# Sums for the modulation vectors on DVE: an order edge on every sum, and a wider spacing

## The chip, the core and the metric

The kernel runs on one NeuronCore of a Trainium2 chip. Time is device time in microseconds of one execution. The engines are named as in the profile: PE (TensorE, matmuls), PEld (its weight loads), DVE (VectorE), ACT (ScalarE), POOL (GpSimd), SP (SyncE, which here only issues DMAs). Each engine works through its own queue in the order in which the program was built, and waits for semaphores where an operand comes from another engine.

## What is computed

Two transformer blocks of two layers each, on 512 tokens of width 1024, in float32. What matters here is the feed-forward sublayer of the first block and the modulation vectors of the second:

```
def _swiglu(h, w_in, w_out):                       # first block, layers 0 and 1
    gu = h @ w_in
    return (jax.nn.silu(gu[..., :FFN_HIDDEN]) * gu[..., FFN_HIDDEN:]) @ w_out

# second block, for its layers l = 0, 1:
sc, sc_ctx = jax.nn.silu(c), jax.nn.silu(c_ctx)
mod   = split_cols((sc @ w_mod[l] + b_mod[l])[:, None, :], (D_MODEL,) * N_MOD)
mod_x = split_cols(sc_ctx @ w_mod[l] + b_mod[l], (D_MODEL,) * N_MOD)
```

FFN_HIDDEN is 2816, N_MOD is 6. The modulation of the second block depends on `c` and `c_ctx` alone, not on the tokens, so it may be computed at any earlier time. `w_mod[l]` is 1024 x 6144.

## The kernel before, in words

**The feed-forward sublayer** (`ffn_core`). The 2816 hidden columns are 22 tiles of 128, in three groups of 8, 8 and 6. For a tile `j`, PE multiplies two slabs of weights (gate and up, each split into a high and a low part, `whia`/`wloa` or `whib`/`wlob`) with the activations `xh`, `xl`: 48 matmuls into one PSUM buffer `b` of 128 x 1024. There are two such buffers. `post` then makes the hidden values: ACT takes a tanh of the gate half into `th`, DVE makes `(th + 1) * gate` (`scalar_tensor_tensor`) and `th * up` (`tensor_mul`), and after the second the PSUM buffer is free (`psB.rel`). So PE can start tile `j + 2` only when both DVE operations of tile `j` are done. ACT and POOL then split `th` into `hh` and `hl`. Behind the tiles of a group comes the product with the output weights, in two halves `h` of 512 columns, four token blocks each, in the same PSUM buffers; DVE adds the results to `x` (`evac`, seen as `x<-b,x`), and PE's second half needs the buffers of the first.

**The modulation** (`modulation`). Layer `l` of it runs as a stream of its own beside the feed-forward sublayer of layer `l` of the first block. It does not use PE for its large product: for each of six vectors `j`, and each of eight slabs of 128 rows of `w_mod` (512 KB each, loaded by ACT's DMA queue into one of three buffers `mw`), DVE multiplies the slab with one value of `c` per partition and adds it to the accumulator `macc` (128 x 1024). The first slab of a vector is a `tensor_scalar`, the other seven are a `scalar_tensor_tensor`; here they are called sums, all of them. For layer 0 both `c` and `c_ctx` are wanted for all vectors (96 sums), for layer 1 both for the first two and one for the rest (64 sums). Then the accumulator is reduced: a blockwise transpose (`mtr`), a reduction (`mpart`), a small matmul on PE (`s<-mpart,quart`), and an addition into `modc` or `mcol`. The load of slab `i` can only be issued when the sums on slab `i - 3` have released their buffer, and it is issued by ACT, whose queue also holds the casts of the feed-forward weights and the tanh.

**What sets the order.** The program is recorded by a small planner (`Weave`). Each stream is a generator; it is stepped when its planned time `ready` lies behind PE's planned time. An engine operation in a stream adds its estimated cost to `ready`, and the code may add to it by hand: behind each sum stands `w.cur.ready += 1800` (ns), which spreads the sums. After recording, a scheduler places the instructions of every engine in a final order; there, instructions of other streams may move past each other if nothing ties them. `with self.tc.issue_after(ins)` adds such a tie: what is recorded in the block stands behind `ins` in its engine's queue, without a semaphore. Before the change this tie is on the first slab of a vector alone (`k == 0`), and the instruction is the one that `self.normed` held when the stream began: the last subtraction of the normalisation that fills `xh` and `xl` (`split_T`, `self.normed = nc.vector.tensor_sub(...)`). All engine operations go through one helper, so the profile gives the line of that helper, L138, for all of them; operations are told apart by the names of their tiles.

Of the kernel before, what the change touches and what calls it, by code (L numbers as in the profile page):

```python
# [13 lines left out]
ALU = mybir.AluOpType  # L14
# [368 lines left out]
class Build:  # L383
# [765 lines left out]
    def ffn_core(self, wi, wo, segs, pre, setup, evac, nxt, grid=None):  # L1149
# [3 lines left out]
        nc, w, v = self.nc, self.w, self.nc.vector  # L1153
# [13 lines left out]
        def post(j, kk, pb, px, hs):  # L1167
            rth = mem["th"]
            th = yield from rth.take()
            ps = [(pb[:, :512], pb[:, 512:], slice(0, 512))]  # L1170
            if px is not None:
                ps.append((px[:, :256], px[:, 256:], slice(512, 768)))
            for pg, _, t in ps:
                nc.scalar.activation(th[:, t], pg, AF.Tanh, scale=0.5)
            yield
            for pg, _, t in ps:
                v.scalar_tensor_tensor(th[:, t], th[:, t], 1.0, pg, ALU.add, ALU.mult)
            for _, pu, t in ps:
                v.tensor_mul(th[:, t], th[:, t], pu)
            self.psB.rel()  # L1180
            if px is not None:
                self.psM.rel()
            yield
            for (hh, hl), (_, _, t) in zip(hs, ps):
                oh, ol, s = hh[:, kk], hl[:, kk], th[:, t]
                if grid is not None:
                    g = "p (c s n) -> p n s c", "p (n s c) -> p n s c"
                    g = g if grid == "to" else g[::-1]
                    oh, ol = (x.rearrange(g[0], s=2, n=4) for x in (oh, ol))
                    s = s.rearrange(g[1], s=2, n=4)  # L1190
                nc.scalar.copy(oh, s)
                self.sub(ol, s, oh.bitcast(F32), "pool")
            rth.rel()
# [14 lines left out]
        def units(js, gi, k0, cuts):  # L1208
            pbs = [(self.psB.get(), self.psM.get() if len(segs) > 1 else None) for _ in js]
            sl = {}  # L1210
            end = cuts[-1][1]
            for c0, c1, need in cuts:
                w.join(*need)
                for j, (pb, px) in zip(js, pbs):
                    for half, m in enumerate("gu"):
                        if (m, j) not in sl:
                            sl[m, j] = self.slabs.get(wi, (m, j))
                        self.mm_a(sl[m, j], outs(half, pb, px, c0, c1))
                        if c1 == end:
                            self.slabs.done(sl[m, j])  # L1220
                    if c1 == end:
                        posts[j] = w.spawn(post(j, j - k0, pb, px, hidden(gi)), 0)
# [4 lines left out]
        for gi, (k0, n) in enumerate(FFN_GROUPS):  # L1227
# [13 lines left out]
            for h in range(1 if last else 2):  # L1241
                acc = self.accs(nb)
# [92 lines left out]
    def modulation(self, l, pool, after):  # L1335

        nc, A, v, w = self.nc, self.A, self.nc.vector, self.w
        for s in after:
            yield s
        normed = self.normed  # L1340
        bm = pool.tile([128, 6, 8], F32, name="bm", tag="bm", bufs=1)
        nc.scalar.dma_start(bm, A["bmod_col"][l])
        wm = {}

        def load(i):
            if i < 48:
                j, k = divmod(i, 8)
                wm[i] = pool.tile([128, 1024], F32, name="mw", tag="mw", bufs=3)
                t = w.cur.ready
                nc.scalar.dma_start(wm[i], A["w_mod"][l, k * 128:k * 128 + 128,  # L1350
                                                      j * 1024:j * 1024 + 1024])
                w.cur.ready = t

        load(0)
        load(1)
        w.cur.ready += 5000
        for j in range(6):
            n_v = 2 if l == 0 or j < 2 else 1
            acc = pool.tile([128, 2, 1024], F32, name="macc", tag="macc", bufs=1)
            for k in range(8):  # L1360
                load(8 * j + k + 2)
                wt = wm.pop(8 * j + k)
                for s in range(n_v):
                    cs = self.cv[:, s, k:k + 1]
                    if k == 0:
                        with self.tc.issue_after(normed.ins):
                            v.tensor_scalar(acc[:, s], wt, cs, None, ALU.mult)
                    else:
                        v.scalar_tensor_tensor(acc[:, s], wt, cs, acc[:, s], ALU.mult, ALU.add)
                    w.cur.ready += 1800  # L1370
                    yield
            w.cur.ready += 5000
            yield

            part = pool.tile([128, 2, 32], F32, name="mpart", tag="mpart", bufs=1)
            for s in range(n_v):
                tr = pool.tile([128, 1024], F32, name="mtr", tag="mtr", bufs=1)
                v.transpose(tr, acc[:, s])
                yield
                v.tensor_reduce(part[:, s], tr.rearrange("p (i q) -> p i q", q=32), AX.X, ALU.add)  # L1380
                yield
            n = 8 * n_v
            pt = yield from self.psS.take()
            ps = pt[:, :n].rearrange("p (s k) -> p s k", s=n_v)
            for q in range(4):
                nc.tensor.matmul(ps[32 * q:32 * q + 32], self.quart,
                                 part[:, :n_v].rearrange("p s (k q) -> p q s k", q=4)[:, q],
                                 start=True, stop=True)
            yield
            if j in (2, 5):  # L1390
                col = pool.tile([128, 2, 8], F32, name="mcol", tag="mcol", bufs=1)
                v.tensor_add(col[:, :n_v], ps, bm[:, j].unsqueeze(1).to_broadcast([128, n_v, 8]))
                yield
                nc.tensor.transpose(pt[:n, 128:256], col[:, :n_v].rearrange("p s k -> p (s k)"), self.ident)
                yield
                gr = pool.tile([16, 128], F32, name="gr", tag="gr", bufs=1)
                nc.scalar.copy(gr[:n], pt[:n, 128:256])
                self.psS.rel()
                yield
                nc.scalar.dma_start(self.grow[l, j // 3, :n_v].rearrange("s (k c) -> (s k) c", k=8), gr[:n])  # L1400
                yield
            else:
                jj = {0: 0, 1: 1, 3: 2, 4: 3}[j]
                for s in range(n_v):
                    v.scalar_tensor_tensor(self.modc[:, l, jj, s], ps[:, s], 1.0 if jj % 2 else 0.0,
                                           bm[:, j], ALU.add, ALU.add)
                self.psS.rel()
                yield
# [1167 lines left out]
```

## Time and profile before

| | |
|---|---|
| median of 3 runs | 3430.48 us (3426.53 to 3433.2) |
| profiled execution | 3435.41 us, its span 3433.6 us |
| PE busy | 3123.7 us, 91% of the span |
| DVE busy | 1735.3 us, 51% |
| ACT, POOL busy | 1257.0 us (37%), 1440.1 us (42%) |
| mean granted clock of TensorE | 0.947 |
| chain of waits | PE 67%, DVE 23%; `macc` alone 5% |
| all sums with their opening products | 270.5 us of DVE: 140 of 1812 ns, 20 of 1166 ns |

The span runs from the first to the last instruction. The feed-forward sublayer of layer 0 begins at about 440 us of it, that of layer 1 at about 1210 us. DVE is busy for half of the span on average, but in 440 to 640 us for 179.0 of 200 us. A busy share of PE counts matmuls whose ends are modelled; a wait is read from the idle time in front of an instruction, and what ended it.

### The profile page before, as it was taken

What the parts mean: (1) busy time and instruction counts of PE and PEld (TensorE: products, weight loads), DVE (VectorE), ACT (ScalarE), POOL (GpSimd) and SP (SyncE); (2) the same over time, 40 slices, a digit from 0 to 9 for tenths busy, and PEclk for the clock granted to TensorE, in tenths of its full rate; (3) what the DMA queues carried; (4) which work ended last, traced back from release to release, by engine and by line L of the source; (5) the groups of instructions that cost most, each with busy time, mean ns of one, the idle gap of its engine ahead of it and who ended that gap; (6) DMA issues with size and microseconds to landing.
All of it is one profiled execution on the core that took longest, in us unless ns stands there. A gap on an engine that the chain in (4) does not pass through costs nothing.

```text
span 3433.6 us, 44377 instructions
## 1 busy us (share of the span) xinstructions
PE 3123.7 (91%) x16596; PEld 2696.9 (79%) x16596; DVE 1735.3 (51%) x4221; ACT 1257.0 (37%) x2542; POOL 1440.1 (42%) x987
## 2 busy tenths in 40 slices
PE   7889888999999979999899897999998799869998
PEld 5678767777998767788788777888886789758886
DVE  6975598543464697213644755121015855751113
ACT  4443322222454422333455635212122555543322
POOL 2313344554323245555523325434445534355555
PEclk9989989999999989999999899999999899889999
DMA  3111255432222267323101212111111111242221
GB/s 106 63 33 62 87 178 172 158 122 95 68 63 68 74 210 244 124 94 118 51 24 44 74 41 80 62 65 65 62 67 53 52 39 54 66 122 94 98 98 68
DMA packets 99449, 301.82 MB, mean 88 GB/s; under 512 B 18673, under 2 KB 26017, under 8 KB 99233
## 3 DMA queue, kind: packets, MB, share of 16 engines
q1 hardware_dynamic: 74000, 236.36, 20.3%
q10 hardware_dynamic: 25232, 62.62, 5.7%
q8 instruction: 131, 2.15, 0.3%
q14 instruction: 86, 0.70, 0.1%
HBM read 290.98 MB, written 7.95 MB: 87 GB/s over the span
## 4 chain that ended last, share of the span: by engine, by line
PE 67%; DVE 23%; issue 4%; ACT 3%; DMA 2%; POOL 1%; ACTq 0%; SPq 0%; DVEq 0%; POOLq 0%
PE b L138 37%; PE m L138 24%; PE s L138 6%; DVE macc L138 5%; DVE rs_t L138 4%; DVE x L138 2%; DVE four L138 1%; ACT xn L138 1%; DMA mw<-w_mod 1%; DVE w2k L138 1%; DVE qrs L138 1%; DVE cx L138 1%; DVE tmp L138 1%; DVE T L138 1%; DVE th L138 1%
## 5 line engine op out<-in xcount | busy, mean ns | idle before, releaser
L138 POOL TENSOR_TENSOR wloa<-wrawa,whia 128x1024 fp32r<-128x1024 f32 (+2 forms) x164 | 391.9, 2391 | 617.8 <-ACT whia L138 375.3
L138 DVE SCALAR_TENSOR_TENSOR th<-th,b 128x512 f32<-128x512 f32 x88 | 60.3, 685 | 720.3 <-ACT th L138 720.3
L138 POOL TENSOR_TENSOR wlob<-wrawa,whib 128x1024 fp32r<-128x1024 f32 (+1 forms) x123 | 297.7, 2423 | 301.2 <-ACT whib L138 191.2
L138 ACT CAST whia<-wrawa 128x1024 fp32r<-128x1024 f32 (+2 forms) x164 | 168.3, 1027 | 401.8 <-PE b L138 162.0
L138 PE MATMUL b<-xh,whib 128*128 128x512 f32 (+1 forms) x768 | 288.6, 381 | 24.2 <-DVE th L138 16.8
L138 PE MATMUL b<-xh,whia 128*128 128x512 f32 (+1 forms) x768 | 286.7, 379 | 14.1 <-DVE th L138 12.1
L138 PE MATMUL b<-xl,whia 128*128 128x512 f32 (+1 forms) x768 | 285.2, 377 | 2.0 <-POOL xl L138 2.0
L138 PE MATMUL b<-xl,whib 128*128 128x512 f32 (+1 forms) x768 | 286.7, 379 | 0.0
L138 DVE SCALAR_TENSOR_TENSOR macc<-mw,cv,macc 128x1024 f32<-128x1024 f32 x140 | 247.9, 1812 | 16.1 <-DMA mw<-w_mod 15.6
L138 ACT CAST whib<-wrawa 128x1024 fp32r<-128x1024 f32 (+1 forms) x123 | 125.7, 1022 | 327.8 <-PE b L138 164.5
L138 POOL TENSOR_TENSOR wloa<-wrawb,whia 128x1024 fp32r<-128x1024 f32 (+2 forms) x61 | 141.6, 2321 | 189.5 <-ACT whia L138 120.2
L138 PE MATMUL m<-xh,whia 128*128 128x512 f32 (+2 forms) x520 | 188.3, 367 | 23.6 <-DVE T L138 10.1
L138 POOL TENSOR_TENSOR wlob<-wrawb,whib 128x1024 fp32r<-128x1024 f32 (+1 forms) x61 | 149.8, 2456 | 131.3 <-ACT whib L138 85.4
L138 POOL TENSOR_TENSOR hl<-th,hh 128x512 fp32r<-128x512 f32 (+1 forms) x110 | 151.8, 1389 | 101.4 <-ACT hh L138 97.0
L138 PE MATMUL b<-xh,wlob 128*128 128x512 f32 (+1 forms) x768 | 194.0, 373 | 0.0
L138 PE MATMUL b<-xh,wloa 128*128 128x512 f32 (+1 forms) x768 | 192.2, 372 | 0.0
L138 PE MATMUL m<-xl,whia 128*128 128x512 f32 (+2 forms) x520 | 184.9, 360 | 3.0 <-POOL xl L138 2.9
L138 PEld LDWEIGHTS b<-xh,whib 128*128 128x128 f32 x768 | 148.0, 193 | 47.3 <-issue 11.9
L138 PEld LDWEIGHTS b<-xh,whia 128*128 128x128 f32 x768 | 147.1, 191 | 36.4 <-issue 13.6
L138 PE MATMUL m<-whib,xh 128*128 128x512 f32 (+3 forms) x432 | 162.6, 379 | 13.8 <-ACT xh L138 12.8
L138 PE MATMUL m<-whia,xh 128*128 128x512 f32 (+3 forms) x440 | 170.8, 392 | 4.6 <-ACT xh L138 2.8
L138 PE MATMUL m<-whia,xl 128*128 128x512 f32 (+3 forms) x440 | 167.3, 383 | 0.4 <-DVE xl L138 0.3
(459 smaller groups left out, 8025.7 us busy)
## 6 DMA issues: line engine op xcount, KB each, us to landing
mw<-w_mod ACTq DMA_DIRECT2D x96, 512.0 KB, 4.3
wrawa<-ffn_w_in SPq DMA_DIRECT2D x60, 512.0 KB, 3.3
wrawa<-w_ffn_in SPq DMA_DIRECT2D x56, 512.0 KB, 3.3
wrawa<-gdn_w_in SPq DMA_DIRECT2D x32, 512.0 KB, 3.3
wrawb<-w_ffn_in SPq DMA_DIRECT2D x32, 512.0 KB, 3.3
wrawa<-w_ffn_out SPq DMA_DIRECT2D x32, 512.0 KB, 3.3
wrawb<-ffn_w_in SPq DMA_DIRECT2D x28, 512.0 KB, 3.3
wrawa<-ffn_w_out SPq DMA_DIRECT2D x28, 512.0 KB, 3.3
```

Of the source, the lines that this page charges most:

```text
L138: r = f(*a, **k)
```

## The change

It does two things, both in `modulation`, with one line in `ffn_core` for it. `self.normed` is now also set by the `tensor_mul` on `th` in `post`, so it always names the newest such product (or the normalisation's subtraction, before the first); and every sum, not only the first of a vector, is recorded behind what `self.normed` holds at that moment. And the time that the planner adds behind each sum is 2300 ns in place of 1800.

```
             for _, pu, t in ps:
-                v.tensor_mul(th[:, t], th[:, t], pu)
+                self.normed = v.tensor_mul(th[:, t], th[:, t], pu)
...
-        normed = self.normed
...
                     cs = self.cv[:, s, k:k + 1]
-                    if k == 0:
-                        with self.tc.issue_after(normed.ins):
+                    with self.tc.issue_after(self.normed.ins):
+                        if k == 0:
                             v.tensor_scalar(acc[:, s], wt, cs, None, ALU.mult)
-                    else:
-                        v.scalar_tensor_tensor(acc[:, s], wt, cs, acc[:, s], ALU.mult, ALU.add)
-                    w.cur.ready += 1800
+                        else:
+                            v.scalar_tensor_tensor(acc[:, s], wt, cs, acc[:, s], ALU.mult, ALU.add)
+                    w.cur.ready += 2300
```

DVE at the first tiles of the feed-forward sublayer of layer 0, before (`macc<-mw,cv` is the opening product of a vector, `macc<-mw,cv,macc` a sum; the two operations on `th<-th,b` are those of `post`):

```order
L138 TENSOR_SCALAR macc<-mw,cv 128x1024 x2
L138 SCALAR_TENSOR_TENSOR macc<-mw,cv,macc 128x1024 x9
L138 SCALAR_TENSOR_TENSOR th<-th,b 128x512
L138 SCALAR_TENSOR_TENSOR macc<-mw,cv,macc 128x1024 x2
L138 TENSOR_TENSOR th<-th,b 128x512
L138 SCALAR_TENSOR_TENSOR macc<-mw,cv,macc 128x1024 x2
L138 SCALAR_TENSOR_TENSOR th<-th,b 128x512
L138 SCALAR_TENSOR_TENSOR macc<-mw,cv,macc 128x1024
L138 STREAM_TRANSPOSE mtr<-macc 128x1024
L138 TENSOR_TENSOR th<-th,b 128x512
```

The same place after:

```order
L138 TENSOR_SCALAR macc<-mw,cv 128x1024 x2
L138 SCALAR_TENSOR_TENSOR macc<-mw,cv,macc 128x1024
L138 SCALAR_TENSOR_TENSOR th<-th,b 128x512
L138 TENSOR_TENSOR th<-th,b 128x512
L138 SCALAR_TENSOR_TENSOR macc<-mw,cv,macc 128x1024 x2
L138 SCALAR_TENSOR_TENSOR th<-th,b 128x512
L138 TENSOR_TENSOR th<-th,b 128x512
L138 SCALAR_TENSOR_TENSOR macc<-mw,cv,macc 128x1024 x4
L138 SCALAR_TENSOR_TENSOR th<-th,b 128x512
L138 TENSOR_TENSOR th<-th,b 128x512
L138 SCALAR_TENSOR_TENSOR macc<-mw,cv,macc 128x1024 x3
```

The two operations on `th` of a tile now stand side by side, with at most a few sums between one tile's pair and the next; one sum in place of nine stands ahead of the first pair.

DVE at the end of the first group of eight tiles of the same sublayer, before: the last pair on `th`, then what stands ahead of the evacuations of the output product's first half (`x<-b,x`):

```order
L138 SCALAR_TENSOR_TENSOR th<-th,b 128x512
L138 TENSOR_TENSOR th<-th,b 128x512
L138 SCALAR_TENSOR_TENSOR modc<-s,bm 128x8 x2
L138 TENSOR_REDUCE mpart<-mtr 128x32
L138 STREAM_TRANSPOSE mtr<-macc 128x1024
L138 TENSOR_REDUCE mpart<-mtr 128x32
L138 TENSOR_SCALAR macc<-mw,cv 128x1024 x2
L138 SCALAR_TENSOR_TENSOR macc<-mw,cv,macc 128x1024
L138 SCALAR_TENSOR_TENSOR x<-b,x 128x512 x2
```

The same place after:

```order
L138 SCALAR_TENSOR_TENSOR th<-th,b 128x512
L138 TENSOR_TENSOR th<-th,b 128x512
L138 SCALAR_TENSOR_TENSOR macc<-mw,cv,macc 128x1024 x7
L138 STREAM_TRANSPOSE mtr<-macc 128x1024
L138 TENSOR_REDUCE mpart<-mtr 128x32
L138 STREAM_TRANSPOSE mtr<-macc 128x1024
L138 TENSOR_REDUCE mpart<-mtr 128x32
L138 TENSOR_SCALAR macc<-mw,cv 128x1024 x2
L138 SCALAR_TENSOR_TENSOR macc<-mw,cv,macc 128x1024 x3
L138 SCALAR_TENSOR_TENSOR x<-b,x 128x512 x2
```

Ten sums stand where one stood, and all of the reduction of a vector.

ACT at the third and fourth tanh of that sublayer after the change (`DMA mw<-w_mod` is the issue of a slab's load, `whib`/`whia` are casts of feed-forward weights):

```order
L138 DMA mw<-w_mod 128x1024
L138 CAST whib_3326<-wrawb_3325 128x1024
L138 DMA mw<-w_mod 128x1024
L138 CAST whib_3328<-wrawa_108 128x1024
L138 ACTIVATE th<-b 128x512
L138 CAST hh_3701<-th 128x512
L138 DMA mw<-w_mod 128x1024
L138 CAST whia_111<-wrawa_107 128x1024
L138 DMA mw<-w_mod 128x1024
L138 CAST whia_109<-wrawb_3325 128x1024
L138 ACTIVATE th<-b 128x512
```

A load still stands in front of most casts, as before; ahead of the third tanh six loads are issued where ten were.

## Rows read from the trace of the kernel before

**Rows 1.** waits of PE, 440 to 800 us: total us, times, longest

```profile
PE b L138 <- DVE th L138: 23.4, 8, 5.7
PE s L138 <- DVE mpart L138: 2.9, 1, 2.9
PE b L138 <- DVE x L138: 2.2, 2, 1.3
```

**Rows 2.** waits of PE, 1250 to 1420 us

```profile
PE b L138 <- DVE th L138: 19.3, 4, 7.2
PE b L138 <- DVE x L138: 5.8, 1, 5.8
```

**Rows 3.** timeline of DVE, three stretches: start, us, operation, count

```profile
465.52 4.51 DVE L138 SCALAR_TENSOR_TENSOR macc<-mw,cv,macc 128x1024 f32<-128x1024 f32 x2
469.95 0.67 DVE L138 TENSOR_TENSOR th<-th,b 128x512 f32<-128x512 f32 x1
...
577.18 1.27 DVE L138 SCALAR_TENSOR_TENSOR x<-b,x 128x512 f32<-128x512 f32 x2
...
583.76 13.23 DVE L138 SCALAR_TENSOR_TENSOR macc<-mw,cv,macc 128x1024 f32<-128x1024 f32 x11
```

**Rows 4.** timeline of PE, three stretches; in brackets idle time before, and releaser

```profile
470.77 0.76 PE L138 MATMUL b<-xh,whib 128*128 128x512 f32 x1 [5.67 <-DVE th L138]
...
474.30 0.40 PE L138 MATMUL b<-xh,whib 128*128 128x512 f32 x1
474.53 0.39 PE L138 MATMUL b<-xl,whib 128*128 128x512 f32 x1
...
553.38 0.77 PE L138 MATMUL b<-whib,hh 128*128 128x512 f32 x1 [4.88 <-DVE th L138]
...
1383.28 0.77 PE L138 MATMUL b<-xh,whib 128*128 128x512 f32 x1 [5.79 <-DVE x L138]
```

**Rows 5.** table by windows: busy us of each engine, granted clock, DMA

```profile
465.00:478.00 13.00, 7.33 (x26) 5.85 (x26) 13.00 (x9) 3.44 (x5) 6.94 (x3) 0.74 0.64 210
```

**Rows 6.** timeline of ACT and DVE at tiles without sums

```profile
659.73 0.60 ACT L138 ACTIVATE th<-b 128x512 f32<-128x512 f32 x1 [0.78 <-PE b L138]
...
661.08 0.69 DVE L138 TENSOR_TENSOR th<-th,b 128x512 f32<-128x512 f32 x1
...
671.96 0.69 DVE L138 TENSOR_TENSOR th<-th,b 128x512 f32<-128x512 f32 x1
```

**Rows 7.** groups of DVE: busy us, mean ns of one, idle before

```profile
L138 DVE SCALAR_TENSOR_TENSOR macc<-mw,cv,macc 128x1024 f32<-128x1024 f32 x140 | 247.9, 1812 | 16.1 <-DMA mw<-w_mod 15.6
L138 DVE STREAM_TRANSPOSE mtr<-macc 128x1024 f32<-128x1024 f32 x20 | 24.8, 1239 | 0.3
L138 DVE TENSOR_REDUCE mpart<-mtr 128x32 f32<-128x1024 f32 x20 | 24.2, 1211 | 0.2
L138 DVE TENSOR_SCALAR macc<-mw,cv 128x1024 f32<-128x1024 f32 x20 | 22.6, 1166 | 0.1
```

**Rows 8.** the tile macc, min/median/max ns; waits of DVE, 1250 to 1420 us

```profile
L138 DVE SCALAR_TENSOR_TENSOR macc<-mw,cv,macc x140: 1239/1280/3435, 449.2 to 1388.7; 128x1024 f32<-128x1024 f32 x140
...
DVE macc L138 <- DMA mw<-w_mod: 15.1, 8, 3.9
```

**Rows 9.** timeline of POOL, first and last of six operations, 553 to 576 us

```profile
553.96 1.29 POOL L138 TENSOR_TENSOR hl<-th,hh 128x512 fp32r<-128x512 f32 x1 [2.41 <-ACT hh L138]
...
572.46 2.39 POOL L138 TENSOR_TENSOR wloa<-wrawa,whia 128x1024 fp32r<-128x1024 f32 x1 [2.33 <-ACT whia L138]
```

**Rows 10.** waits of ACT, 440 to 800 us; the page's group of casts

```profile
ACT whib L138 <- DVE macc L138: 29.6, 6, 12.5
...
L138 ACT CAST whia<-wrawa 128x1024 fp32r<-128x1024 f32 (+2 forms) x164 | 168.3, 1027 | 401.8 <-PE b L138 162.0
```

**Rows 11.** timeline of SP's queue and of DVE, 810 to 840 us

```profile
813.99 10.23 SPq L138 DMA_DIRECT2D wrawa<-dil_w_in  x2
...
836.55 1.28 DVE L138 SCALAR_TENSOR_TENSOR xn<-x,rs,row 128x1024 f32<-128x1024 f32 x1
```

## The prediction

> **What bounds the kernel now.** I read the busy shares and the chain of waits first: TensorE (PE) carries two thirds of the chain, and the next largest share is DVE, a good part of it in `macc`, the running sums of the modulation. The sums run only beside the two feed-forward sublayers of the first block, roughly 440 to 725 us and 1220 to 1392 us, so I then asked for the waits of PE in these two stretches alone. In the first, PE waited 23.4 us for `th`, 2.9 us for `mpart` and 2.2 us for `x`, 28.5 us together [rows 1]; in the second 19.3 us for `th` and 5.8 us for `x`, 25.1 us [rows 2]. All these are DVE's products, all stand where sums are in DVE's queue, and PE's timeline of both stretches has no longer waits on anything else.
>
> The timeline of DVE shows the mechanism [rows 3]: the first operation on a tile's `th` is done at 465.5, two sums of together 4.51 us follow, and only at 469.95 comes the product that frees the PSUM buffer; PE's next tile starts at 470.77 after a wait of 5.67 us [rows 4]. A wait like this has a second price. In 465 to 478 us the granted clock was 0.74 [rows 5], and the eight matmuls from 470.77 to 474.30 took 3.53 us, where the pace behind them is 0.23 us each, 1.84 us for eight [rows 4]: PE stood, fell to the 1.2 GHz level, and lost 1.7 us more. Eight waits of the two stretches are followed by such slow matmuls (those whose first matmul lasts 0.76 us or more; the first and the last of them in [rows 4]): 8 x 1.7 = 13.6 us.
>
> So the sums now cost 28.5 + 25.1 + 13.6 = 67.2 us. More than that the change cannot give back by this way.
>
> **The change part by part.** *The order edge on every sum.* Before, only the first sum of a vector was tied, and to the normalisation. Now each of the 160 sums stands behind the newest `tensor_mul` of `th` that the program had issued. DVE's order shows the effect: the pair on `th` is never split, and 2 to 4 sums follow each pair instead of up to nine ahead of one. No instruction is added; the edge is an order on one queue. What it must not do is make `th` late. Without sums, tanh of a tile starts at 659.73 and the pair is through at 661.77, that is 2.04 us after the tile's last matmul, and the tiles follow each other every 10.88 us (661.08 to 671.96) [rows 6]. PE may go on without a wait when the pair of tile j is done before tile j+1 ends. Four sums at their mean of 1.81 us and the pair, 1.4 us, make 8.6 us; four sums with two transposes and two reductions make 4 x 1.81 + 2 x (1.24 + 1.21) + 1.4 = 13.5 us [rows 7], 2.7 us over the period, once per vector, within the 8.8 us that the pair has in hand. Inside the groups of tiles I therefore put all waits at nothing. The cover is that margin; if it were gone the waits of [rows 1] would stand again.
>
> *What is late next.* At the end of a group of eight tiles DVE must evacuate `x`, because PE's second half of the output product takes the same PSUM buffers. The first half took 553.38 to 577.18, less the 1.7 us of the slow clock 22.1 us [rows 3, 4]. In the new order the following stands on DVE between the last pair of `th` and the first two evacuations (1.27 us):
> - first sublayer, first group: 10 sums, 2 opening products (1.17 us), 2 transposes, 2 reductions: 2.04 + 18.1 + 2.3 + 4.9 + 1.3 = 28.6 us, PE waits 6.5 us;
> - first sublayer, second group: the same and two small additions: 6.8 us;
> - second sublayer, first group: 9 sums, 1 product, 4.9 us: 25.7 us, a wait of 3.6 us;
> - second sublayer, second group: 8 sums, 1 product, 1 reduction, 2 transposes: 22.8 us, 0.7 us.
>
> Together 17.6 us. In the second sublayer the sums for the last four vectors use each slab of weights once, and DVE waited 15.1 us for `mw` there [rows 8]; of these 32 sums 12 stand in the last two lists, so 15.1 x 12/32 = 5.7 us more. Four waits of some size, each with 1.7 us of slow clock: 6.8 us. The change gives back 17.6 + 5.7 + 6.8 = 30.1 us.
>
> The uncertain factor is how long a sum lasts. They take 1.28 us at the median and up to 3.435 us, with a mean of 1.81 [rows 7, 8]; the long ones lie beside a subtraction on POOL. With no such meeting the first list is 2.04 + 12.8 + 2.3 + 4.9 + 1.3 = 23.3 us, the others 23.5, 20.9 and 18.5, and the waits are 1.2 and 1.4 us: 3 us given back. In the same place before, six POOL operations started between 553.96 and 572.46 [rows 9]; if each lengthens one sum by 3.435 - 1.28 = 2.15 us, every list grows to its shortest plus 12.9 us, and the four waits are 14.1, 14.3, 11.7 and 9.3 us: 49.4 + 5.7 + 6.8 = 61.9 us. I take the mean, since it was measured over all 140 sums beside the same POOL work, and keep 3 and 62 us as ends.
>
> The Trainium skill, "GPSIMD Engine Reference", Key points, says that GpSimd shares its SBUF interfaces with VectorE and contends with DVE instructions that have two SBUF inputs, as these sums do; the spread of 1.28 to 3.435 us agrees. By that rule spreading the sums over more tiles lets them meet more of POOL's work, which speaks against the change and for the end of 62 us; by the mean of the rows it is 30.1 us.
>
> *2300 for 1800.* The planner's step from one sum to the next grows by 0.5 us, so fewer are traced per tile and the 96 sums of the first sublayer end some 48 us of PE time later. In the new order the last vector of the first sublayer is complete ahead of the third group's last evacuations, that of the second within its second group; nothing is queued behind them that PE needs sooner. Cost nothing; if the last vector slipped further, the end of the sublayer would wait for it.
>
> *What is moved past other queues.* ACT issues the loads of `mw`, each waiting for the sums on the slab three before, and casts and tanh stand behind them: `whib` alone waited 29.6 us for `macc` in the first stretch [rows 10], under cover of PE. This stays so; its risk is the third rival. On SP the load of `row` now stands behind two loads of `dil_w_in`, which were issued by 824.2, while `row` was first used at 836.55 [rows 11]: hidden by 12 us. Some small DVE operations in the second block change places with each other; no row prices that, and I take 0, within 7 us either way (the spread of the three runs, 3426.5 to 3433.2).
>
> **Sum.** -67.2 + 30.1 = -37.1 us. The profiled execution took 3435.41 us, 1.8 us of it outside its span, so it would become 3398; it lay 4.9 us above the median, and from the median of 3430.5 the forecast is 3394 us.
>
> **Rivals.**
> 1. *The ends of the groups cost nothing.* If the sums there meet little of POOL (the eleven from 583.76 took 13.23 us [rows 3], 1.2 us each) nearly all of the 67 us stays: 3366 us. Against it: this stretch is the only long one of that pace.
> 2. *The wait moves to the evacuations.* With the upper end, 62 us given back, 3425 us; with 7 us for the rest of the kernel up to 3432. For it: POOL has work in just that place [rows 9], and `x` already holds PE for 5.79 us once [rows 4]. Against: this needs every POOL operation to meet a sum.
> 3. *ACT's queue closes a loop, and the kernel is slower.* A pair of `th` is followed by sums, a load waits for them, two casts of 1.03 us [rows 10] and the next tanh stand behind the load. If the load waits for the fourth sum behind the pair, at the 2.26 us that two sums between the operations on `th` took [rows 3], the loop is 2.04 + 9.0 + 2.1 = 13.1 us, 2.2 us over the period of 10.88, in each of some 32 tiles with sums: 70 us on top of 3394, 3464 us. It decides from the point where the awaited sums exceed 10.88 - 4.1 = 6.8 us, three long ones. Against it: a load waits for the slab three before, and by ACT's new order that is the first or second sum behind the pair.
>
> **How the numbers follow.** My forecast, with a range of its own of 3376 to 3412, has 0.58; rival 1 0.14, rival 2 0.18, rival 3 0.10. The range that leaves out 2 in 10 goes from 3364 to 3427: it takes in rival 1 down to 2 us below its own value and most of rival 2. A difference under 0.2%, 7 us, cannot be told from none here. Faster by more: the forecast, rival 1 and half of rival 2, 0.81; within 0.2%: most of the other half, 0.08; slower: rival 3 and a remainder, 0.11.
>
> **What would show it.** PE's waits for `th` within the groups gone, its granted clock near 1.0 between 440 and 540 us; four waits of PE for `x` of 1 to 7 us at the ends of the first and second groups; the sums' mean near 1.8 us and their last one some 50 to 90 us later in each sublayer. I am wrong if PE still waits for `th` or for ACT's casts inside the groups, if the four waits are all near zero or above 10 us, or if the stages after 1420 us change their length by more than 7 us.

## The result, and the profile after

The changed kernel takes 3380.6 us (median of 4 runs, 3377.7 to 3385.9) against 3431.4 us before (4 runs, 3426.5 to 3433.2): a ratio of 0.9856, with an interval of 0.9839 to 0.9873. Its profiled execution took 3381.8 us, 53.6 us less than that of before. The forecast was 3394.

First the waits of PE in the first sublayer, then in the second (total us, times, longest). They answer to [rows 1, 2]:

```profile
PE b L138 <- DVE x L138: 10.0, 2, 6.8
...
PE b L138 <- DVE x L138: 5.7, 2, 3.6
```

All twelve waits for `th`, 42.7 us, are gone. What is left are four waits for `x`. The timeline of PE has them one by one (start, us, operation, idle time and releaser in brackets), the two of the first sublayer and then the two of the second:

```profile
555.69 0.47 PE L138 MATMUL b<-whib,hh 128*128 128x512 f32 x1 [3.22 <-DVE x L138]
...
695.96 0.77 PE L138 MATMUL b<-whib,hh 128*128 128x512 f32 x1 [6.82 <-DVE x L138]
...
1300.98 0.47 PE L138 MATMUL b<-whib,hh 128*128 128x512 f32 x1 [2.06 <-DVE x L138]
...
1436.77 0.77 PE L138 MATMUL b<-whib,hh 128*128 128x512 f32 x1 [3.61 <-DVE x L138]
```

They are the ends of the first two groups of each sublayer, 15.7 us in all. Behind three of them (not behind the one of 2.06 us) seven or eight matmuls on `b` take 0.55 us or more, 22 in all, where 71 did before.

The table by windows over the stretch of [rows 5] and over the first 100 us of the sublayer (busy us of PE, PEld, DVE, ACT, POOL; granted clock; DMA):

```profile
465.00:478.00 13.00, 13.00 (x59) 10.76 (x58) 12.45 (x7) 3.08 (x4) 9.74 (x5) 1.00 0.56 193
440.00:540.00 100.00, 99.54 (x539) 85.88 (x539) 76.87 (x58) 27.91 (x36) 56.64 (x24) 1.00 0.48 157
```

PE is busy for all 13 us where it was for 7.33, and the granted clock is 1.00 (the upper level, 2.4 GHz, throughout) where it was 0.74. DVE's timeline at the same tiles, which answers to [rows 3], shows why:

```profile
459.73 0.69 DVE L138 SCALAR_TENSOR_TENSOR th<-th,b 128x512 f32<-128x512 f32 x1 [9.55 <-ACT th L138]
460.46 0.69 DVE L138 TENSOR_TENSOR th<-th,b 128x512 f32<-128x512 f32 x1
461.06 5.06 DVE L138 SCALAR_TENSOR_TENSOR macc<-mw,cv,macc 128x1024 f32<-128x1024 f32 x2
466.04 0.67 DVE L138 SCALAR_TENSOR_TENSOR th<-th,b 128x512 f32<-128x512 f32 x1
466.75 0.69 DVE L138 TENSOR_TENSOR th<-th,b 128x512 f32<-128x512 f32 x1
```

The pair on `th` is one piece, 1.4 us, and DVE now waits for ACT's tanh instead of the other way round. At the end of the first group it reads:

```profile
531.97 0.69 DVE L138 TENSOR_TENSOR th<-th,b 128x512 f32<-128x512 f32 x1
532.58 9.78 DVE L138 SCALAR_TENSOR_TENSOR macc<-mw,cv,macc 128x1024 f32<-128x1024 f32 x7
...
547.21 3.55 DVE L138 TENSOR_SCALAR macc<-mw,cv 128x1024 f32<-128x1024 f32 x2
550.68 3.67 DVE L138 SCALAR_TENSOR_TENSOR macc<-mw,cv,macc 128x1024 f32<-128x1024 f32 x3
554.27 1.28 DVE L138 SCALAR_TENSOR_TENSOR x<-b,x 128x512 f32<-128x512 f32 x2
```

The list ahead of the evacuations is the one forecast, ten sums and a vector's reduction, but these ten sums took 13.45 us by the two lines above. Single records overlap a little; by the mean of their durations, the measure by which the forecast had 1.81 us, it is 1.41 us each. Over the whole kernel a sum takes longer than before (the page's group: busy us, mean ns; it answers to [rows 7]), with min/median/max ns from the view of the tile (to [rows 8]):

```profile
L138 DVE SCALAR_TENSOR_TENSOR macc<-mw,cv,macc 128x1024 f32<-128x1024 f32 x140 | 267.7, 1954 | 9.3 <-DMA mw<-w_mod 8.6
```

```profile
L138 DVE SCALAR_TENSOR_TENSOR macc<-mw,cv,macc x140: 1266/1567/3425, 448.9 to 1432.9; 128x1024 f32<-128x1024 f32 x140
```

**Where the 53.6 us are.** These two marks cut the span: a sublayer begins with its first matmul `b<-xh,whib` and is taken to its last two evacuations `x<-b,x`. In the changed kernel:

```profile
436.45 0.58 PE L138 MATMUL b<-xh,whib 128*128 128x256 f32 x1
...
802.73 1.29 DVE L138 SCALAR_TENSOR_TENSOR x<-b,x 128x512 f32<-128x512 f32 x2 [1.43 <-PE b L138]
...
1181.00 0.58 PE L138 MATMUL b<-xh,whib 128*128 128x256 f32 x1 [0.68 <-ACT xh L138]
...
1543.63 1.29 DVE L138 SCALAR_TENSOR_TENSOR x<-b,x 128x512 f32<-128x512 f32 x2 [0.24 <-PE b L138]
```

Before, the same marks stand at 436.92, 828.46, 1212.19 and 1601.49. The same cut through the profile of every kernel of this study, us:

| kernel | ahead | sublayer 1 | between | sublayer 2 | rest | span |
|---|---|---|---|---|---|---|
| before | 436.9 | 391.5 | 383.7 | 389.3 | 1832.1 | 3433.6 |
| after | 436.4 | 366.3 | 378.3 | 362.6 | 1836.4 | 3380.0 |
| after, again | 436.7 | 366.0 | 378.8 | 362.2 | 1836.1 | 3379.8 |
| edge, 1800 | 436.6 | 366.7 | 378.3 | 361.5 | 1828.7 | 3371.8 |
| edge, 1800, again | 433.2 | 366.4 | 381.8 | 361.4 | 1828.5 | 3371.4 |
| spacing 2300 alone | 432.6 | 386.4 | 378.4 | 373.7 | 1831.1 | 3402.1 |
| no sums | 432.9 | 364.3 | 379.8 | 363.8 | 1830.4 | 3371.2 |
| no sums, no loads | 428.6 | 352.7 | 381.4 | 355.0 | 1834.9 | 3352.5 |
| no POOL subtractions | 432.9 | 357.2 | 365.3 | 358.5 | 1838.0 | 3351.8 |
| held, 1400 | 434.3 | 352.5 | 381.1 | 354.8 | 1836.6 | 3359.2 |
| held, 1400, again | 434.4 | 352.8 | 385.0 | 354.7 | 1836.6 | 3363.5 |
| held, 1200 | 425.7 | 355.7 | 381.1 | 362.0 | 1837.7 | 3362.2 |
| held, 1000 | 434.1 | 359.8 | 381.7 | 359.9 | 1830.8 | 3366.3 |
| held, 2300 | 434.4 | 352.4 | 398.9 | 353.7 | 1837.3 | 3376.7 |

The change gives 25.2 us in the first sublayer and 26.7 in the second, 51.9 together; what lies outside (-0.5, -5.4 and +4.3) nearly cancels. In three kernels run twice the sublayers come back within 0.4 us, while the stretches "ahead" and "between" differ by up to 4 us between two executions of the same kernel. So the sublayers' columns are the ones to compare kernels by. Each row is the one execution that was profiled, which can lie off its kernel's median: 3403.9 against 3412.3 us for the spacing alone, 3353.6 against 3344.1 without POOL's subtractions.

PE's busy time divides the gain. The table by windows over the two sublayers, before, after, and in "no sums, no loads", where nothing of the stream holds PE (experiment 4):

```profile
436.92:828.46 391.54, 362.31 (x1683) 298.94 (x1683) 241.40 (x204) 95.21 (x115) 194.66 (x84) 0.97 0.44 146
1212.19:1601.49 389.30, 363.41 (x1698) 302.05 (x1699) 181.26 (x193) 115.34 (x129) 202.53 (x87) 0.96 0.45 153
...
436.45:802.73 366.28, 355.46 (x1682) 295.81 (x1682) 251.32 (x204) 95.22 (x115) 195.20 (x84) 0.98 0.48 156
1181.00:1543.63 362.63, 356.08 (x1690) 297.14 (x1691) 188.21 (x190) 111.47 (x121) 201.16 (x85) 0.99 0.51 165
...
428.57:781.26 352.69, 351.91 (x1683) 293.51 (x1683) 89.88 (x121) 95.91 (x115) 177.36 (x84) 1.00 0.30 99
1162.65:1517.66 355.01, 354.28 (x1702) 296.07 (x1703) 84.16 (x136) 116.72 (x133) 189.97 (x88) 1.00 0.32 107
```

PE's idle time (the stretch less the first figure behind it) is 55.1 us before, 17.4 after and 1.5 without the stream; its busy time is 725.7, 711.5 and 706.2 us, at a granted clock of 0.96 to 0.97, 0.98 to 0.99, and 1.00. So 37.7 us of the gain are waits, and 14.2 us are matmuls that got shorter at the higher clock.

### The profile page after: what moved, and what is told of

It is laid out like the page before. It is cut to its first block, busy times and chain, and to the rows that moved or that the text cites. A ratio compares the mean times of both kernels' runs of the same rounds, so it can differ in the third digit from the quotient of the medians.

```text
span 3380.0 us, 44351 instructions
## 1 busy us (share of the span) xinstructions
PE 3112.0 (92%) x16596; PEld 2693.0 (80%) x16596; DVE 1749.6 (52%) x4221; ACT 1257.0 (37%) x2542; POOL 1438.3 (43%) x987
## 4 chain that ended last, share of the span: by engine, by line
PE 54%; DVE 12%; ACT 3%; issue 1%; DMA 1%; POOL 1%; ACTq 0%; SPq 0%; DVEq 0%; POOLq 0%
PE b L138 33%; PE m L138 17%; PE s L138 4%; DVE rs_t L138 3%; DVE x L138 1%; ACT xn L138 1%; DVE four L138 1%; DVE w2k L138 1%; DVE macc L138 1%; DVE qrs L138 1%; ACT w2k L138 0%; DVE xn L138 0%; DVE bst L138 0%; DVE cx L138 0%; DVE rs L138 0%
## 5 line engine op out<-in xcount | busy, mean ns | idle before, releaser
L138 DVE SCALAR_TENSOR_TENSOR macc<-mw,cv,macc 128x1024 f32<-128x1024 f32 x140 | 267.7, 1954 | 9.3 <-DMA mw<-w_mod 8.6
L138 POOL TENSOR_TENSOR hl<-th,hh 128x512 fp32r<-128x512 f32 (+1 forms) x110 | 159.1, 1455 | 63.1 <-ACT hh L138 63.1
L138 PE MATMUL m<-whib,xh 128*128 128x512 f32 (+3 forms) x432 | 162.3, 378 | 13.5 <-ACT xh L138 13.1
L138 PE MATMUL m<-whib,xl 128*128 128x512 f32 (+3 forms) x432 | 161.1, 376 | 2.3 <-POOL xl L138 2.3
```

What stands on the lines that cost most here:

```text
L138: r = f(*a, **k)
```

## Experiments

Theory: the sums cost time only by what stands behind them on DVE; the edge frees `th`, and what it gives back is PE's four waits for `x`. Its rivals: the wider spacing does it; the sums have a cost that no wait shows; the ends of groups are held by something else.

**1. The edge alone** (`edge_1800`, run twice).

```
-                    w.cur.ready += 2300
+                    w.cur.ready += 1800
```

> The order edge alone, with the planner's step left at 1800. Theory (the edge is what frees the tiles, and what is given back is only PE's waits for x at the ends of groups): no wait for th, as with the whole change. Ahead of the first evacuations stand 7 and 11 sums (first sublayer) and 7 and 5 (second), where the whole change has 10, 10 to 12, 9 and 8; at the 1.95 us a sum that the changed kernel shows, the waits are about 2, 7, 1 and 0 us, 10 in all, where the whole change has 15.7: 3375 us, 3368 to 3385. Rival (the wider spacing is needed, since four or five sums behind every pair are too many for a tile's 10.88 us): waits for th come back in most tiles with sums, 3400 us or more.

Measured: 3373.6 us (3371.5 to 3374.9), ratio to before 0.983 (0.9812 to 0.9848). PE's waits, first sublayer, then second:

```profile
PE b L138 <- DVE x L138: 9.6, 2, 5.5
...
PE b L138 <- DVE x L138: 3.9, 1, 3.9
```

No wait for `th`: the edge needs no wider spacing. The waits for `x` are 13.5 us where I expected 10; the sublayers take what they take in the changed kernel (366.7 and 361.5 us). The 7 us less lie in "rest". Run again beside the changed kernel, it gave:

> The edge with 1800 once more beside the changed kernel. The two sublayers took 367.3 and 362.1 us with it, 366.9 and 363.2 us in the changed kernel; the 7 us between the two times lie behind them. Theory (the spacing does nothing to the sublayers, and the 7 us are the planner's other order where the second block begins, so they stay): 3374 us, 5 to 9 us under the changed kernel. Rival (they are a matter of the run): the two within 3 us.

> The changed kernel once more, on the same chip as the others of this call, to compare them directly: 3381 us, 3375 to 3387.

Measured in one call: 3372.8 us (3365.1 to 3373.3) with 1800, 3379.5 (3372.2 to 3381.6) with 2300, ratios to before of 0.9825 (0.9806 to 0.9844) and 0.9849 (0.983 to 0.9869). The medians lie 6.7 us apart again. The two intervals overlap, but "rest" shows the same in all four traces: 1828.7 and 1828.5 us with 1800, 1836.4 and 1836.1 with 2300. Of these 7.6 us, 5 arise in the 60 us behind the last evacuation of the second sublayer, where PE's interleaved order of the next normalisation's transposes differs. That this order is the cause was not tried by itself.

**2. The spacing alone**: the kernel before, with 2300.

> The spacing alone: 2300, and the edge on the first slab of a vector only, as before. Theory (the edge does it): sums still split the pair on th in most tiles with sums, PE's waits for th stay at 30 us or more in the two sublayers, and the time stays near before, 3415 to 3440. Rival (thinning the sums does it): the waits for th fall to a few us and the time is near that of the whole change, 3380 to 3395.

Measured: 3412.3 us (3403.9 to 3414.0), ratio 0.9939 (0.9917 to 0.996). PE's waits, first sublayer, then second:

```profile
PE b L138 <- DVE x L138: 11.2, 2, 6.2
PE b L138 <- DVE th L138: 9.7, 4, 3.7
PE b L138 <- ACT th L138: 2.4, 1, 2.4
...
PE b L138 <- DVE th L138: 13.5, 3, 7.3
```

Between the two: a little under my range. As many pairs are split as before, 13 in either kernel, but 23.2 us of waits for `th` behind DVE are left of 42.7, and 2.4 behind ACT; the waits for `x` are 11.2 us in the first sublayer where they were 2.2, and 0.3 in the second where they were 5.8. What makes fewer of the split pairs late was not looked for. The sublayers get 20.7 of the change's 51.9 us shorter: thinning the sums gives two fifths of the gain there (by the medians 0.6% of the whole time, where the change gives 1.4%); only the order gives all of it.

**3. No sums**: the changed kernel without its 140 sums.

```
-                        else:
-                            v.scalar_tensor_tensor(acc[:, s], wt, cs, acc[:, s], ALU.mult, ALU.add)
```

> The changed kernel without the 140 sums of slabs two to eight (the opening product, the loads, the transposes and reductions stay), so the modulation vectors hold the first slab alone. Theory (what the sums still cost is PE's four waits for x, 15.7 us, and two slow starts behind them of 1.7 us): 19 us less than the changed kernel, 3362 us, 3355 to 3368; the whole price of the sums before was then about 69 us, by my forecast 67. Rival A (the sums cost more than PE's named waits, by lengthening POOL's subtractions and holding ACT's casts): below 3350. Rival B (the waits for x would be there in any case, since something else holds the evacuations): within 5 us of 3381.

Measured: 3376.2 us (3373.1 to 3377.1), ratio 0.9839 (0.9818 to 0.986): hardly better than with the sums. Rival B had this number, but not this cause: the waits for `x` are gone, and others stand in their place. PE's waits in the first sublayer, then ACT's:

```profile
PE b L138 <- DVE th L138: 6.4, 2, 3.7
PE b L138 <- ACT xh L138: 2.0, 1, 2.0
PE b L138 <- ACT whia L138: 1.0, 1, 1.0
...
ACT whib L138 <- DMA mw<-w_mod: 38.8, 5, 10.5
...
ACT whia L138 <- DMA mw<-w_mod: 26.7, 4, 8.2
```

DVE had no sums to do, yet `th` was late: ACT, which issues the loads of `mw`, stood at them until earlier loads into the same three buffers had landed, and casts and tanh stood behind. This is near the third rival of the prediction, where casts and tanh stand behind loads; but here the loads waited for a landing and not for sums. It says nothing on the price of the sums, so:

**4. No sums and no loads.** The edit of experiment 3, and in addition only one of each vector's eight slabs is loaded.

```
-            if i < 48:
+            if i < 48 and i % 8 == 0:
```

> As the kernel without the 140 sums, and the loads of their slabs left out too (one slab of eight is loaded and multiplied, so the modulation vectors hold that slab alone). In the kernel that left out the sums alone, ACT's casts waited 50 us for loads of mw to land between 440 and 560 us, and PE 6.4 and 5.4 us for th. Theory (those waits came from loads issued in a row on ACT's queue, once no sums spread them): without the loads PE waits for neither th nor x in the two sublayers, and the time is that of the kernel with held sums less what it still waits for the last vector at the end of the first sublayer (5.6 + 3.8 us): 3351 us, 3344 to 3358. Rival A (the waits for th come from tanh and casts themselves): 3368 to 3378. Rival B (the sums have a cost that no wait of PE shows): below 3340.

Measured: 3359.5 us (3354.3 to 3363.8), ratio 0.98 (0.978 to 0.982), 1.5 us above the range; the list of PE's waits is empty for 440 to 800 and for 1190 to 1440 us. The sublayers take 352.7 and 355.0 us. That is the floor (experiment 6 comes to the same with all the sums in place), and by it the sums and loads cost 38.8 + 34.3 = 73.1 us before and 13.6 + 7.6 = 21.2 us in the changed kernel. Experiment 3 lies 20.4 us above it: that is what the loads on ACT's queue cost when no sums space them.

**5. Sums that do not meet POOL.** POOL's subtractions for the feed-forward weights of the first block are left out, and TensorE takes the high part in place of the low one.

```
+                if arr.startswith("ffn_w"):
+                    self.ready[self.split] = ((arr, key), (hi, lo, hi), nk, e)
+                else:
+                    b.sub(lo[:, :e], raw[:, :e], hi[:, :e].bitcast(F32), lo_eng)
...
```

> The changed kernel without POOL's subtractions for the feed-forward weights of the first block; TensorE takes the high part a second time in place of the low part, so the low parts' share of those products is wrong, the matmuls are as many. Theory (a sum is 1.27 us alone and 2.2 to 2.4 us when it meets one of these subtractions, and that is what makes the lists ahead of the evacuations longer than PE's half product): the sums' mean falls from 1.95 to 1.3 us, the lists get 3 to 7 us shorter, PE's waits for x fall from 15.7 us to about 4 us (what is left is the wait for mw of 3.5 us), one slow start of 1.7 us goes: 3367 us, 3360 to 3373. Rival A (the sums' length has another cause, such as their loads writing into SBUF): mean stays at 1.9, 3376 to 3386. Rival B (the lists are short of time whatever a sum takes): mean 1.3, but waits for x stay over 10 us.

Measured: 3344.1 us (3341.9 to 3353.6), ratio 0.9761 (0.9739 to 0.9783). The sums and opening products (min/median/max ns), and PE's waits for `x`, first sublayer, then second:

```profile
L138 DVE SCALAR_TENSOR_TENSOR macc<-mw,cv,macc x140: 1270/1277/2668, 446.9 to 1404.8; 128x1024 f32<-128x1024 f32 x140
L138 DVE TENSOR_SCALAR macc<-mw,cv x20: 741/746/748, 445.6 to 1389.2; 128x1024 f32<-128x1024 f32 x20
```

```profile
PE b L138 <- DVE x L138: 0.5, 1, 0.5
...
PE b L138 <- DVE x L138: 2.8, 1, 2.8
```

The mean of a sum falls to 1.47 us (POOL still splits `th`), no opening product is longer than 0.75 us, and the waits for `x` fall from 15.7 to 3.3 us: the theory's 4. The sublayers get 13.2 us shorter. That is about what I expected; the time falls by more. In the profiled executions "between" gets 13.0 us shorter too, and most of that is idle time of PE, 30.2 us in the changed kernel and 19.5 here; I had not counted that, and its cause was not tried. The median lies another 9.5 us under the profiled execution, and where those are no trace shows.

**6. Sums held until the evacuations are recorded** (`hold_1400`, run twice). The first line below stands behind a group's last tile; the second place is `evac`, the third the loop over the sums.

```
+            self.hold = len(segs) == 1
...
-            v.scalar_tensor_tensor(xs, ps, 0.5, xs, ALU.mult, ALU.add)
+            self.normed = v.scalar_tensor_tensor(xs, ps, 0.5, xs, ALU.mult, ALU.add)
+            if not h and b == 3:
+                self.hold = False
...
-                    w.cur.ready += 2300
+                    w.cur.ready += 1400
                     yield
+                    if self.hold:
+                        yield lambda: not self.hold
```

> The changed kernel, and in addition no sum is recorded from a group's last tile until the four evacuations of its first half of the output product have been, and the evacuations set the mark that later sums stand behind; the step is 1400, so that the sums are still done in time. In DVE's order no sum stands between the last pair of a group and its evacuations any more. Theory (the ends of groups cost 15.7 us of waits and 3.4 us of slow clock): PE's waits for x go to zero, 3362 us, 3355 to 3370. Rival A (the denser sums inside the groups make th late): waits for th of 10 us or more in all, 3370 to 3400. Rival B (the sums pushed behind the evacuations come too late for the next ones or for the end of the sublayer): waits for x or at the end of the sublayer, no gain over 3381.

Measured: 3360.8 us (3359.0 to 3362.3), ratio 0.9793 (0.9775 to 0.9811). DVE at the end of the first group:

```profile
529.57 0.69 DVE L138 TENSOR_TENSOR th<-th,b 128x512 f32<-128x512 f32 x1
547.20 1.29 DVE L138 SCALAR_TENSOR_TENSOR x<-b,x 128x512 f32<-128x512 f32 x2 [16.94 <-PE b L138]
549.92 1.29 DVE L138 SCALAR_TENSOR_TENSOR x<-b,x 128x512 f32<-128x512 f32 x2 [1.43 <-PE b L138]
551.12 6.58 DVE L138 SCALAR_TENSOR_TENSOR macc<-mw,cv,macc 128x1024 f32<-128x1024 f32 x4
```

DVE idles 16.94 us there, and PE waits for `x` 0.4 us in both sublayers together. They take 352.5 and 354.8 us, which is the floor: with this order all the sums are hidden. Repeated beside the changed kernel:

> The held sums with 1400 once more beside the changed kernel: 3361 us, 3356 to 3366, 15 to 25 us under the changed kernel of this call. Rival: the first result was a lucky phase of the first 440 us, which differ by up to 10 us from kernel to kernel; then 3365 to 3372.

Measured: 3367.5 us (3365.3 to 3370.2), ratio 0.9819 (0.9801 to 0.9837), 12 us under the changed kernel of that call. The sublayers are the same to 0.3 us; "between" is 4 us longer than in the first execution. So the first result did flatter it, and the rival's time was right; its place was not, since the first 440 us took the same (434.3 and 434.4 us). Still, the slowest run of this version is under the fastest of the changed kernel (3370.2 against 3372.2 us).

**7. How dense, how late.** Steps of 1200, 1000 and 2300 with the sums held.

> The held sums with a step of 1200 in place of 1400: the last vector of the first sublayer is complete on DVE's queue behind the pair of the third group's fourth tile, not at its end. Theory: PE's waits of 5.6 us for mcol and 3.8 us for xn at the end of the first sublayer go, everything else stays: 3351 us, 3345 to 3357. Rival (up to five sums with transposes and reductions in a tile of 10.88 us make th late, or ten sums between the evacuations of the two halves make the second late): waits for th or x of 5 us or more come back, 3358 to 3375.

> The held sums with a step of 1000: the last vector of the first sublayer is complete behind the pair of the third group's third tile, and up to five sums follow a pair. Theory: as with 1200, no waits for mcol or xn, 3351 us, 3345 to 3357. Rival (five sums at 2 us, the pair at 1.4 us and a vector's reduction of 4.9 us make 16.3 us where a tile has 10.88, and two such tiles in a row use up the 8.8 us in hand): waits for th of 3 to 10 us, 3355 to 3370.

> The held sums with the step of the change, 2300. Held for 22 us at each group's end and spaced wider, the last vector of the first sublayer is late: behind the last evacuations of the third group's first half, DVE's queue still has 15 sums, two opening products, and two vectors' reductions, some 30 to 40 us, mixed with the evacuations x<-m and the operations of the next normalisation. Theory (a wide step costs nothing until the last vector runs over the last group, and from there on it sets the end): the stretch from the last evacuation x<-b of the first sublayer to the first tile of the second gets 10 to 30 us longer, 3371 to 3391 us. Rival (the vectors are wanted only in the second block, so being late costs nothing): as with 1400, 3356 to 3366.

Measured: 3365.2 us (3358.3 to 3370.5), ratio 0.9817 (0.9791 to 0.9843), with 1200; 3362.3 (3360.4 to 3368.1), 0.9812 (0.9792 to 0.9831), with 1000; 3379.3 (3377.2 to 3383.0), 0.9854 (0.9836 to 0.9872), with 2300. PE's waits for `th`, 1200 (first sublayer, then second), then 1000 (first):

```profile
PE b L138 <- DVE th L138: 2.6, 1, 2.6
...
PE b L138 <- DVE th L138: 4.9, 1, 4.9
```

```profile
PE b L138 <- DVE th L138: 5.0, 1, 5.0
```

Both rivals came true: the sublayers are 3 to 7 us over the floor. The waits for `th` stand at the end of the first group, where four sums and one or two transposes with their reductions stand between two pairs and use up the 8.8 us in hand. In the second sublayer with 1000 PE waits for `mpart` instead, 3.8 us. And the waits of 5.6 and 3.8 us behind the first sublayer, which I wanted to save, gave nothing: "between" is 381 us with or without them, since others took their place. With 2300 the sublayers are at the floor, but the last vector is late:

```profile
825.10 0.31 PE L138 MATMUL s<-mpart,quart 128*32 128x16 f32 x8 [22.30 <-DVE rs_t L138]
```

PE waits 22.3 us behind the first sublayer. Its matmul reads `mpart`, the last vector's reduction, and ahead of that DVE had 15 sums from the last evacuation on, in between the next normalisation's small operations (one of which the trace names as the releaser); "between" is 14 to 18 us longer than with 1400.

## Why the prediction was right

Faster was the likeliest case, by the mechanism that the experiments show, and 3380.6 us lies in the forecast's own range of 3376 to 3412, 5 us from its lower end. (The sum gives 3393.4, which I put down as 3394.) By its steps:

- **The price of the sums before, 67.2 us.** By the floor it was 73.1. The waits were right: 53.6 us is PE's idle time over the floor (55.1 less 1.5). The slow clock was put too low: PE's busy time was 19.5 us over the floor (725.7 against 706.2), not 13.6. The eight slow starts were not all of eight matmuls; 6 to 13 were slow behind each, 71 in all, which makes some 16 us. Where the last 4 lie stays open.
- **No wait for `th` within the groups.** Right: 0 us, and the granted clock is 1.00 in 440 to 540 us. Experiments 1 and 2 show that the edge does this, and that the margin of 8.8 us, which I named as the cover, is real: it is used up in experiment 7. The last sum came 70 and 75 us later in its sublayer than before, as forecast.
- **The waits for `x`: 17.6 us, then 5.7 for slabs, then 6.8 of slow clock; 30.1 given back.** The mechanism and its four places were right, the term was too large and is the step that failed: 21.2 us by the floor, of which 15.9 are idle time and 5.3 slower matmuls. The four waits were to be 6.5, 6.8, 3.6 and 0.7 us and were 3.2, 6.8, 2.1 and 3.6. In the first list of either sublayer the sums took 1.41 and 1.47 us, not 1.81; in the second lists, 1.83 and 1.77, they came out as forecast. The 5.7 us for slabs were counted on top of the four waits, and are 3.5 us inside the last of them; DVE stood twice in that list:

```profile
1421.89 3.95 DVE L138 SCALAR_TENSOR_TENSOR macc<-mw,cv,macc 128x1024 f32<-128x1024 f32 x2 [1.17 <-DMA mw<-w_mod]
...
1429.50 4.67 DVE L138 SCALAR_TENSOR_TENSOR macc<-mw,cv,macc 128x1024 f32<-128x1024 f32 x2 [2.33 <-DMA mw<-w_mod]
...
1435.38 1.25 DVE L138 SCALAR_TENSOR_TENSOR x<-b,x 128x512 f32<-128x512 f32 x2
```

- **A sum's mean of 1.81 us.** It rose to 1.95, since 92 of the 140 sums overlap an operation on POOL where 74 did. Those that meet none take 1.28 us in either kernel, those that do 2.3 us. So the point that I weighed against the change, that spreading the sums lets them meet more of POOL, holds; it costs nothing where the pair on `th` has its margin, and at the ends of groups fewer met POOL than the mean, 17 of 37. A mean over all is not the mean of the place that counts.
- **2300 for 1800 at no cost.** Right for the sublayers (within 1.1 us either way). It costs 7 us behind them, most of it where the second block begins and the planner's order differs; that lies about at the 7 us that I allowed for such changes of place, but it comes back in each trace and is not noise. That a later last vector would set the end is shown by experiment 7.
- **ACT's queue.** Casts waited 82.3 us for `macc` in the first sublayer, 56.7 before (29.6 of it `whib`, [rows 10]), and PE did not wait for them:

```profile
ACT whia L138 <- DVE macc L138: 44.2, 10, 8.2
...
ACT whib L138 <- DVE macc L138: 38.1, 9, 7.3
```

  The loop of the third rival did not close; experiment 3 shows that loads on this queue can make `th` late, by another wait than the one it named.
- **The rivals.** The first (ends of groups at nothing) needed all sums at 1.2 us and came 15 us too low; the second needed every POOL operation to meet a sum, and in the first list POOL met both opening products (the two took 3.55 us, 1.4 where they meet nothing) and three of the ten sums.

The gain was put 6 us too small and the part given back 9 us too large. Both make the forecast too slow, so no error hid another; they are the 15 us between the forecast's -37 and the sublayers' -52.

## What to carry to other kernels

When a bulk stream shares an engine with a short operation that frees a buffer, tie the stream behind that operation, piece by piece; here a wider fixed step alone left as many pairs split as before. Then look where the short operation changes: here each group ended in another one, the evacuation, that the edge did not name, and it got nearly all the waits that were left. Find the floor by leaving the stream out together with its loads, since loads without their readers hold up the queue that issues them.

## What the runs showed of the hardware

An operation on DVE met by POOL is lengthened by kind, not by size. In the changed kernel a sum (two operands in SBUF) goes from 1.27 us to as much as 3.43; an opening product, which reads one tensor, from 0.74 to 2.89; but no transpose or reduction of the same 128 x 1024 takes over 1.25 us, though 31 of the 40 overlap POOL. The Trainium skill, "SBUF — State Buffer", Summary: rules for kernel authors, has it that a DVE instruction with two SBUF inputs, or in a mode that uses two ports, and one of GpSimd exclude each other (with two inputs, when GpSimd's reads SBUF): the second to issue stands until the first is through. The opening product at 547.87 us agrees, with 2.89 us of which 2.34 lie beside one of POOL's subtractions; that it runs in such a mode no row shows. It goes both ways: POOL's subtractions of 128 x 1024 took 2.67 us on average beside a sum or an opening product, and 2.41 us without (440 to 1440 us of the changed kernel).
